# A hybrid encoder trunk: the planner's VectorE costs are refitted

## The chip, the cores and the metric

The kernel runs on one core of one Trainium2 chip, as one program. The metric is device time in microseconds (us) for one execution; the time of a kernel is the median of its runs. The core has TensorE (PE, matrix products, with a queue of its own for loading weights, PEld), VectorE (DVE), ScalarE (ACT), GpSimd (POOL) and SyncE (SP, which only issues DMAs here). Every engine works its own list of instructions in a fixed order and waits on semaphores for what another engine has to deliver.

## The reference

An encoder trunk of two layers on 512 tokens of width 1024, with a memory of 256 tokens. Each layer has four sub-layers, each between a norm ahead of it and a norm behind it:

```python
def rms_norm(x, w):
    xf = x.astype(jnp.float32)
    y = xf * lax.rsqrt(jnp.mean(xf * xf, axis=-1, keepdims=True) + NORM_EPS)
    return (y * w.astype(jnp.float32)).astype(x.dtype)

def swiglu(u, w_gate, w_up, w_down):
    return (jax.nn.silu(u @ w_gate) * (u @ w_up)) @ w_down

# each layer
#   x += 1/2 * postnorm(SwiGLU(prenorm(x)))
#   x +=       postnorm(W_out[ret_heads | gdn_heads](prenorm(x)))
#   x +=       postnorm(CrossAttn(prenorm(x), norm(mem)))
#   x += 1/2 * postnorm(SwiGLU(prenorm(x)))
```

The second sub-layer, called the mixing sub-layer below, has four heads of retention in both directions with rotated queries and keys, and four heads of a gated delta rule whose chunks need a triangular inverse. Everything is float32, and the feed-forward width is 2816.

## The kernel before, in words

**Products.** Each float32 operand of a projection is cut into a high and a low part (`cut`: ScalarE copies the high part, VectorE subtracts it to get the low one), and a product is three matmuls, high by high, high by low and low by high. `uH` and `uL` are the parts of the normalised input `u`, turned so that the model dimension lies on the partitions; `wts` (and `wx` during a transition) are the parts of the weights, cut from the 1 MB blocks `raw` that SyncE loads; `ps` are the eight PSUM banks. These projections run one after the other on TensorE and are called the stream.

**The transition** (`transition`, line 822; `chain`, 758) leads from one sub-layer to the next. The 512 tokens are four tiles of 128, numbered 0 to 3. The output projection finishes tile by tile, and for each tile a thread then does the following:
1. VectorE weighs the output with the post-norm's weights, both halves of 512 columns (`tmp<-ps,wpost`), while ScalarE takes its sum of squares (`junk<-ps`).
2. The inverse root of the mean square (`rsqrt`, small operations on 128x1 tiles `sm`).
3. VectorE updates the residual, half by half (`x<-tmp,sm,x`), and ScalarE takes the sum of squares of each new half (`junk<-x`).
4. A second inverse root, now for the next sub-layer's pre-norm.
5. VectorE makes the next input, half by half (`tmp<-x,sm,wpre`). For each half four transposes on TensorE follow (`ps<-ident,tmp`), and then the cut (`uH<-ps`, `uL<-ps,uH`).

Two tables say which engine takes the roots: `POST_DVE = (3,)` has VectorE take the first root of tile 3 alone, and `PRE_DVE = (0, 1, 3)` has it take the second root of tiles 0, 1 and 3. So both roots of tile 2 are done by GpSimd, 11 operations each (13 with the two that add and scale). The threads' priorities are `PRIO = (-1, -1, 13, -1)`: tile 2 comes last.

Meanwhile the stream goes on with the next sub-layer's first projections (`first_group`, line 734): first for the columns of tiles 0 and 1 (half 0), which need only those two tiles, then for tiles 2 and 3 (half 1), which need both of the others. So half 0 is the work that TensorE has while tiles 2 and 3 are normalised. There are eight such transitions behind a sub-layer, of which seven lead to another sub-layer; the last one only writes the output.

**The mixing sub-layer.** Retention's rotated queries and keys go to memory (`qkd<-rt`) and are loaded again by head (`q<-qkd`, `k<-qkd`), all on SyncE's queue, which also carries the weights (`raw`) and the decay table (`T<-decd`).

**What sets the order.** Every step is written as a thread that yields one operation after the other. `Sched` (line 200 on) runs all threads in a model when the program is built: it holds a clock for each engine and, for each piece of memory, when and by which engine it was written last. `cost` (line 159) estimates how long an operation takes. `ready` (line 216) says when it may start: the writer's end plus `SAME`, if the writer is the same engine, or plus `OTHER` (0.23). `run` (line 276) then takes, on the engine that can start soonest, the operation of the smallest priority number among those that could start within `WAIT` (0.4 us on VectorE) of the earliest. The operations are emitted in that order, and this is the order in which each engine's list stands on the chip. The figures of the model appear nowhere else: they change which operation stands ahead of which, and neither what is computed nor which engine does it.

On the profile nearly all instructions have line 239, the line of the scheduler that emits them, so the groups are told apart by their tiles.

Of the kernel before, what the change touches and what calls it, by code (L numbers as in the profile page):

```python
# [90 lines left out]
class Op:  # L91


    def __init__(self, eng, calls, rd, wr, cost):
        self.eng, self.calls, self.rd, self.wr, self.cost = eng, calls, rd, wr, cost
        self.ready, self.size = 0.0, 0
        self.table = TABLE.get(calls[0][2].get("func")) if eng == "ACT" else None
# [36 lines left out]
def free_size(ap):  # L134
    n = 1
    for _, c in tuple(ap.ap)[1:]:
        n *= c
    return n


class Eng:
# [5 lines left out]
    def __getattr__(self, name):  # L147
        fn, kind = getattr(self.obj, name), self.kind

        def make(*args, **kw):  # L150
            outs = [kw[k] for k in ("out", "accum_out") if kw.get(k) is not None]
            rest = list(args)
            if "out" not in kw:
                outs.append(rest.pop(0))
            ins = [a for a in rest if isinstance(a, bass.AP)]
            ins += [a for k, a in kw.items() if k not in ("out", "accum_out") and isinstance(a, bass.AP)]
            out = outs[0]
            return Op(kind, [(fn, args, kw)], [cells(a) for a in ins], [cells(a) for a in outs],
                      cost(kind, name, out, ins))
        return make  # L160


def cost(kind, name, out, ins):
    n = free_size(out)
    if name == "dma_start":
        return 0.06
    if kind == "PE":
        if name == "transpose":
            return n / 2400 * 2
        if ins[1].dtype == F32R:  # L170
            return max(n, 256) / 2385 if n >= 256 else 0.213
        return 4 * n / 2400
    n = max([n] + [free_size(a) for a in ins])
    psum = any("PSUM" in str(a.space) for a in [out] + list(ins))
    if kind == "ACT":
        return 0.2 + n * 0.00083
    if kind == "DVE":
        if name in ("tensor_copy", "tensor_scalar", "memset") and not psum:
            return 0.07 + n / 1920
        return (0.13 if psum else 0.07) + n / 960  # L180
    if name == "tensor_tensor":
        return 0.15 + n * 0.0036
    return 0.15 + n * 0.0009
# [7 lines left out]


CODE = {"PE": 0, "ACT": 1, "DVE": 2, "POOL": 3, "SP": 4}
SAME, OTHER = 0.12, 0.23
WAIT = {"PE": 0.25, "ACT": 0.3, "DVE": 0.4, "POOL": 0.2, "SP": 0.0}


class Sched:
# [18 lines left out]
    def ready(self, op):  # L217
        e, t = CODE[op.eng], 0.0
        for c in op.rd:
            w, by, r = self.arrays(c)  # L220
            i = slice(None) if c[2] is None else c[2]
            t = max(t, float((w[i] + np.where(by[i] == e, SAME, OTHER)).max()))
            if c[3]:
                t = max(t, float(r[i].max()) + 0.1)
        for c in op.wr:
            w, by, r = self.arrays(c)
            i = slice(None) if c[2] is None else c[2]
            t = max(t, float(r[i].max()) + 0.1)
            if op.eng != "PE" and (c[2] is not None or c[3]):
                t = max(t, float((w[i] + np.where(by[i] == e, 0.0, OTHER)).max()))  # L230
        op.ready = t
# [259 lines left out]
class Kernel:  # L491
# [372 lines left out]
    def ffn(self, l, i, nxt):  # L864
        sd, st = self.sched, self.st
        with self.pool("ffn") as fp:
            h = self.tile(fp, "h", [KF, S])
            hx = [tuple(self.tile(fp, f"hx{c}", [S], F32R) for c in "HL")]
            made, ready = [], set()
            last = [False]  # L870

            first = (l, i) == self.subs[0]
            self.beside = []
            if first:
                self.scratch = h.rearrange("p a b -> p (a b)")
                self.smalls = {n: self.tile(fp, n, [w]) for n, w in (("wm0", KD), ("wm1", KD), ("ms0", 1), ("ms1", 1), ("ms2", 1),
                                                                     ("lg", 16), ("cr", 2))}
                self.beside = [sd.spawn(g, 45, "beside") for g in (self.memory_in(), self.decays_in())]
            self.gate_up(h, made, ready, last, FAST[l, i], nxt, hx)
            th = self.th  # L880
            if first:
                rot = sd.spawn(self.rotary_in(), 45, "rotary")
            self.transition((l, i), nxt, th, True)
            if first:
                sd.run(lambda: rot.done)

    def gate_up(self, h, made, ready, last, j0, nxt, hx):


        sd, st, V = self.sched, self.st, self.V  # L890
        uH, uL = self.uH, self.uL
        plain, formed, done = [False], [False], [False]
        out = lambda k: h[:, k], list(range(KF)), hx + self.uring(), lambda k: k in ready, lambda: last[0]
        gated = {}

# [1042 lines left out]
```

## Time and profile before

| what | value |
|---|---|
| median of 3 runs | 2420.7 us (2415.57 to 2422.01) |
| the profiled execution's own time | 2418.85 us |
| its span in the trace | 2417.1 us |
| mean granted clock of TensorE | 0.996 |
| TensorE busy | 2369.2 us |
| VectorE busy | 1739.7 us |
| ScalarE busy | 1166.0 us |
| GpSimd busy | 197.0 us |

The span runs from the first instruction to the last; the execution's own time is 1.75 us longer. Timeline rows give the start and the duration in us, the engine, the line, the operation, what it writes and reads, its shape and how many were merged; in brackets the idle time of the engine ahead of it and who ended it. Rows of windows give the stretch and its length, the busy time and number of instructions on TensorE, the weight loads, VectorE, ScalarE and GpSimd, then the granted clock of TensorE (1.00 is full), the DMA engines' share and GB/s. Rows of waits give who waited for whom: total us, times, the longest.

### The profile page before, as it was taken

How to read it: one execution, taken by the hardware profiler on the slowest of the kernel's cores; microseconds unless marked ns; L12 is line 12 of the kernel's file. 1: busy time of each engine (PE TensorE's matmuls, PEld its weight loads, DVE VectorE, ACT ScalarE, POOL GpSimd, SP SyncE). 2: the span in 40 equal slices, each digit the busy share in tenths (PEclk: the TensorE clock that was granted, in tenths of full speed). 3: DMA queues.
4: the chain of work that ended last, by engine and by line, in shares of the span. 5: the costliest groups of instructions: out<-in, count | busy, mean ns of one | idle time of the engine just before them, and what ended most of it. 6: DMA issues, size and time to landing. Idle time of an engine off the chain costs nothing. (4 is left out here: it accounts for less than half of the span.)

```text
span 2417.1 us, 38683 instructions
## 1 busy us (share of the span) xinstructions
PE 2369.2 (98%) x15566; PEld 2115.9 (88%) x15566; DVE 1739.7 (72%) x2765; ACT 1166.0 (48%) x2003; POOL 197.0 (8%) x584
## 2 busy tenths in 40 slices
PE   7999999998999999999999999999899999999998
PEld 7999888886989889998889998888788898899987
DVE  7988857767776568886388885486877665788852
ACT  5655436732444544554245563366324454455631
POOL 1000001311020020000010000113010200100001
PEclk9999999999999999999999999999999999999999
DMA  6533342454334322335213334235543253133330
GB/s 202 166 124 108 127 140 88 113 173 152 100 122 159 110 83 81 112 105 174 87 36 107 121 127 153 71 101 142 163 154 136 88 166 105 36 105 117 123 137 35
DMA packets 231209, 286.89 MB, mean 119 GB/s; under 512 B 29630, under 2 KB 190966, under 8 KB 231030
## 3 DMA queue, kind: packets, MB, share of 16 engines
q1 hardware_dynamic: 229878, 280.23, 36.0%
q10 hardware_dynamic: 1152, 4.19, 0.4%
q8 instruction: 122, 2.00, 0.3%
q14 instruction: 57, 0.47, 0.1%
HBM read 255.00 MB, written 29.39 MB: 118 GB/s over the span
## 5 line engine op out<-in xcount | busy, mean ns | idle before, releaser
L239 PE MATMUL ps<-uH,wts 128*128 128x256 f32 (+1 forms) x4096 | 929.8, 313 | 0.0
L239 PEld LDWEIGHTS ps<-uH,wts 128*128 128x128 f32 x4096 | 683.4, 189 | 48.4 <-issue 1.0
L239 PE MATMUL ps<-uL,wts 128*128 128x256 f32 (+1 forms) x2048 | 638.3, 312 | 0.8 <-DVE uL L239 0.8
L239 DVE TENSOR_TENSOR wts<-raw,wts 128x1024 fp32r<-128x1024 f32 (+1 forms) x361 | 403.6, 1126 | 125.8 <-ACT wts L239 125.4
L239 ACT ACTIVATE wts<-raw 128x1024 fp32r<-128x1024 f32 (+1 forms) x361 | 348.1, 971 | 183.4 <-PE ps L239 90.1
L239 PEld LDWEIGHTS ps<-uL,wts 128*128 128x128 f32 x2048 | 386.0, 188 | 25.0 <-DVE uL L239 1.8
L239 PE MATMUL ps<-wts,uH 128*128 128x512 f32 x1120 | 346.8, 391 | 0.0
L239 ACT ACTIVATE sg<-ps 128x256 f32<-128x256 f32 (+1 forms) x298 | 117.6, 397 | 269.4 <-PE ps L239 264.9
L239 PEld LDWEIGHTS ps<-wts,uH 128*128 128x128 f32 x1120 | 208.8, 188 | 42.5
L239 DVE TENSOR_TENSOR wts<-T,wts 128x1024 fp32r<-128x1024 f32 x140 | 171.5, 1225 | 70.8 <-ACT wts L239 66.6
L239 PE MATMUL ps<-wts,uL 128*128 128x512 f32 x560 | 218.2, 390 | 0.0
L239 ACT ACTIVATE wts<-T 128x1024 fp32r<-128x1024 f32 x140 | 148.2, 1058 | 45.2 <-DVE T L239 44.2
L239 PE MATMUL ps<-wx,uH 128*128 128x512 f32 x480 | 148.2, 390 | 0.0
L239 PEld LDWEIGHTS ps<-wts,uL 128*128 128x128 f32 x560 | 105.1, 188 | 22.2
L239 PE MATMUL ps<-s2H,wts 128*128 128x256 f32 x560 | 107.9, 278 | 2.7 <-ACT sg L239 2.7
L239 POOL TENSOR_SCALAR sm<-sm 128x1 f32<-128x1 f32 (+1 forms) x165 | 39.7, 241 | 849.4 <-ACT junk L239 823.9
L239 ACT ACTIVATE uH<-h 128x512 fp32r<-128x512 f32 x76 | 46.3, 626 | 127.2 <-PE ps L239 126.5
L239 PE MATMUL ps<-s3H,wts 128*128 128x256 f32 x560 | 107.6, 277 | 0.0
L239 PE MATMUL ps<-s1H,wts 128*128 128x256 f32 x560 | 107.5, 277 | 0.0
L239 DVE TENSOR_TENSOR uL<-h,uH 128x512 fp32r<-128x512 f32 x76 | 51.2, 689 | 77.2 <-ACT uH L239 77.2
L239 PEld LDWEIGHTS ps<-wx,uH 128*128 128x128 f32 x480 | 89.8, 188 | 18.5
L239 ACT ACTIVATE junk<-ps 128x512 bf16<-128x512 f32 (+1 forms) x96 | 47.0, 490 | 113.0 <-PE ps L239 99.5
(321 smaller groups left out, 4226.1 us busy)
## 6 DMA issues: line engine op xcount, KB each, us to landing
raw<-in_ffn_up_dram SPq DMA_DIRECT2D x44, 1024.0 KB, 5.2
raw<-in_ffn_down_dram SPq DMA_DIRECT2D x44, 1024.0 KB, 4.9
raw<-in_ffn_gate_dram SPq DMA_DIRECT2D x43, 1024.0 KB, 5.2
raw<-in_w_in_dram SPq DMA_DIRECT2D x32, 1024.0 KB, 6.0
raw<-in_w_out_dram SPq DMA_DIRECT2D x8, 1024.0 KB, 5.7
raw<-in_xattn_q_dram SPq DMA_DIRECT2D x8, 1024.0 KB, 5.3
raw<-in_xattn_k_dram SPq DMA_DIRECT2D x8, 1024.0 KB, 5.2
raw<-in_xattn_v_dram SPq DMA_DIRECT2D x8, 1024.0 KB, 5.0
```

What stands on the lines that cost most here:

```text
L239: fn(*a, **kw)
```

## The change

Three figures of the planner are replaced. An operation on VectorE now has a fixed part of 0.155 us, where it had 0.07 (0.13 if it touches PSUM). For VectorE alone the gap between an operation and one that depends on it on the same engine is 0.03 us, where it was 0.12 for every engine; the other engines keep 0.12. The part that grows with the number of elements stays. No thread, priority, tile or operation is edited.

```diff
@@ -176,8 +176,8 @@
     if kind == "DVE":
         if name in ("tensor_copy", "tensor_scalar", "memset") and not psum:
-            return 0.07 + n / 1920
-        return (0.13 if psum else 0.07) + n / 960
+            return 0.155 + n / 1920
+        return 0.155 + n / 960
     if name == "tensor_tensor":
@@ -191,7 +191,7 @@
 CODE = {"PE": 0, "ACT": 1, "DVE": 2, "POOL": 3, "SP": 4}
-SAME, OTHER = 0.12, 0.23
+SAME, OTHER = np.array([0.12, 0.12, 0.03, 0.12, 0.12]), 0.23
 WAIT = {"PE": 0.25, "ACT": 0.3, "DVE": 0.4, "POOL": 0.2, "SP": 0.0}
@@ -219,7 +219,7 @@
             i = slice(None) if c[2] is None else c[2]
-            t = max(t, float((w[i] + np.where(by[i] == e, SAME, OTHER)).max()))
+            t = max(t, float((w[i] + np.where(by[i] == e, SAME[e], OTHER)).max()))
```

In the program that comes out, the operations stand in another order at many places on all engines. The rows of the transition, where the order on VectorE, ScalarE and TensorE changes in the same way seven times, are shown in the prediction.

## The prediction

> **What bounds the kernel now.** I read the page's engine shares first, then the chain of waits, then the timeline of TensorE at its idle places, with ScalarE, VectorE and GpSimd beside it. The page:
>
> ```profile
> span 2417.1 us, 38683 instructions
> PE 2369.2 (98%) x15566; PEld 2115.9 (88%) x15566; DVE 1739.7 (72%) x2765; ACT 1166.0 (48%) x2003; POOL 197.0 (8%) x584
> ```
>
> TensorE is the bound: 2369.2 of 2417.1 us busy, 48 us idle. No order of the other engines can win more than those 48 us, while every place where TensorE comes to wait is paid in full. The view of waits names who makes it wait:
>
> ```profile
> PE ps L239 <- DVE tmp L239: 18.5, 10, 9.3
> PEld ps L239 <- DMA q<-qkd: 13.5, 2, 6.9
> PE ps L239 <- DMA k<-qkd: 12.7, 2, 6.5
> ```
>
> The ten waits for `tmp` are the transitions between sub-layers: 9.3 us of the 18.5 is the start of the program, the rest mostly seven waits of about 1 us, one in each transition with a sub-layer behind it. The two waits for `q` and `k` are the two mixing sub-layers (the weight-load queue and the matmul queue count the same two). A stretch of plain projections shows the stream's own rate:
>
> ```profile
> 966.40:1026.80 60.40, 60.40 (x536) 60.40 (x535) 53.82 (x67) 35.96 (x56) 0.00 (x0) 1.00 0.36 115
> ```
>
> 536 matmuls of 256 columns in 60.40 us are 0.113 us each, with no idle time and the clock at 1.00, though VectorE is 89% busy. Dearer figures for VectorE can win nothing there.
>
> TensorE in the first and the last of the seven: a wait for `uL`, the transposes of token tile 3, then those of tile 2 behind a wait for `tmp`:
>
> ```profile
> 370.57 0.39 PE L239 MATMUL ps<-uL,wts 128*128 128x256 f32 x1 [0.46 <-DVE uL L239]
> 380.60 1.03 PE L239 MATMUL ps<-ident,tmp 128*128 128x128 f32 x8
> 382.57 1.38 PE L239 MATMUL ps<-ident,tmp 128*128 128x128 f32 x8 [0.94 <-DVE tmp L239]
> 383.71 0.36 PE L239 MATMUL ps<-uH,wx 128*128 128x256 f32 x1
> ...
> 2069.74 0.40 PE L239 MATMUL ps<-uL,wx 128*128 128x256 f32 x1 [0.19 <-DVE uL L239]
> 2079.69 1.05 PE L239 MATMUL ps<-ident,tmp 128*128 128x128 f32 x8
> 2081.74 1.38 PE L239 MATMUL ps<-ident,tmp 128*128 128x128 f32 x8 [1.00 <-DVE tmp L239]
> ```
>
> What makes these waits so short is that tile 2's normalisation runs on GpSimd under the stream. Its chain in the first transition, on ScalarE, GpSimd and VectorE:
>
> ```profile
> 375.93 0.63 ACT L239 ACTIVATE junk<-x 128x512 bf16<-128x512 f32 x1
> 376.46 0.19 ACT L239 ACTIVATION_READ_ACCUMULATOR junk<-x 128x1 f32 x1
> ...
> 381.24 1.09 ACT L239 ACTIVATE uH<-ps 128x512 fp32r<-128x512 f32 x2 [2.63 <-PE ps L239]
> 383.27 1.32 ACT L239 ACTIVATE uH<-ps 128x512 fp32r<-128x512 f32 x2 [0.94 <-PE ps L239]
> ```
>
> ```profile
> 365.11 0.27 POOL L239 TENSOR_SCALAR sm<-sm,sm 128x1 f32<-128x1 f32 x1 [1.91 <-ACT junk L239]
> 368.94 0.19 POOL L239 TENSOR_TENSOR sm<-sm,sm 128x1 f32<-128x1 f32 x1
> 376.75 0.92 POOL L239 TENSOR_SCALAR sm<-sm,sm 128x1 f32<-128x1 f32 x1 [7.62 <-ACT junk L239]
> 380.32 0.59 POOL L239 TENSOR_TENSOR sm<-sm 128x1 f32<-128x1 f32 x1
> 381.54 0.19 POOL L239 TENSOR_TENSOR sm<-sm,sm 128x1 f32<-128x1 f32 x1
> ```
>
> ```profile
> 369.16 0.75 DVE L239 SCALAR_TENSOR_TENSOR x<-tmp,sm,x 128x512 f32<-128x512 f32 x1 [1.43 <-POOL sm L239]
> 374.33 2.08 DVE L239 SCALAR_TENSOR_TENSOR x<-tmp,sm,x 128x512 f32<-128x512 f32 x3
> 376.32 1.22 DVE L239 TENSOR_TENSOR wts<-raw,wts 128x1024 fp32r<-128x1024 f32 x1
> 379.44 1.42 DVE L239 SCALAR_TENSOR_TENSOR tmp<-x,sm,wpre 128x512 f32<-128x512 f32 x2
> 381.77 1.41 DVE L239 SCALAR_TENSOR_TENSOR tmp<-x,sm,wpre 128x512 f32<-128x512 f32 x2 [0.91 <-POOL xp L239]
> 383.10 2.48 DVE L239 TENSOR_TENSOR uL<-ps,uH 128x512 fp32r<-128x512 f32 x4
> ```
>
> GpSimd's inverse root (13 operations) takes 4.98 us here, 376.75 to 381.73, of which TensorE waits 0.94. Its first one in this transition took 4.02 (365.11 to 369.13).
>
> **The change part by part.** *The figures themselves* add no instruction. The new ones fit: the 128x1024 operation above takes 1.22 us, 0.155 + 1024/960 = 1.222 against the old 1.137. But no time follows from a better fit; only the order can bring it.
>
> *The transitions.* A shorter gap between dependent operations lets tile 3's small operations (priority -1) follow each other without a hole, so tile 2's update of `x` (priority 13) no longer gets in between. On VectorE, first transition, `x2_8` and `x3_9` are the residual tiles 2 and 3, `tmp_65` and `tmp_66` their work tiles. Before:
>
> ```order
> L239 SCALAR_TENSOR_TENSOR sm3_92_2620<-sm3_93_2621,sm3_92_2620 128x1
> L239 SCALAR_TENSOR_TENSOR x3_9_105<-tmp_66_2583,sm3_92_2620,x3_9_105 128x512
> L239 SCALAR_TENSOR_TENSOR x2_8_104<-tmp_65_2582,sm2_85_2613,x2_8_104 128x512
> L239 SCALAR_TENSOR_TENSOR x3_9_105<-tmp_66_2583,sm3_92_2620,x3_9_105 128x512
> L239 TENSOR_TENSOR wts_84<-raw1_83,wts_84 128x1024
> ```
>
> Now, behind tile 3's second root:
>
> ```order
> L239 SCALAR_TENSOR_TENSOR tmp_66_2577<-x3_9_105,sm3_96_2615,wpre_68_2579 128x512 x2
> L239 SCALAR_TENSOR_TENSOR x2_8_104<-tmp_65_2576,sm2_85_2604,x2_8_104 128x512
> L239 TENSOR_TENSOR uL_2_92<-ps3_77,uH_1_91 128x4x128
> L239 TENSOR_TENSOR uL_2_92<-ps5_79,uH_1_91 128x4x128
> L239 TENSOR_TENSOR wts_84<-raw1_83,wts_84 128x1024
> L239 TENSOR_TENSOR wts_84<-raw0_82,wts_84 128x1024
> L239 SCALAR_TENSOR_TENSOR tmp_65_2576<-x2_8_104,sm2_89_2608,wpre_68_2579 128x512 x2
> ```
>
> Before, the second half of `x2_8` stands between the halves of `x3_9`, ahead of the weight cut and tile 3's second root (its first half stands 15 rows earlier). Now the first half stands there, and the second behind all of that and behind `tmp_66`. On ScalarE, where the sum of squares of that half (`sm2_89`) is taken, before:
>
> ```order
> L239 ACTIVATE junk_73,sm3_95_2623<-x3_9_105 128x512
> L239 ACTIVATE junk_73,sm2_89_2617<-x2_8_104 128x512
> L239 ACTIVATE junk_73,sm3_96_2624<-x3_9_105 128x512
> L239 DMA xd_85<-x3_9_105 128x1024
> L239 DMA xd_85<-x2_8_104 128x1024
> L239 ACTIVATE wts_84<-raw1_83 128x1024
> L239 ACTIVATE uH_1_91<-ps7_81 128x4x128
> L239 ACTIVATE uH_1_91<-ps4_78 128x4x128
> ```
>
> and now:
>
> ```order
> L239 ACTIVATE junk_73,sm2_88_2607<-x2_8_104 128x512
> L239 ACTIVATE junk_73,sm3_96_2615<-x3_9_105 128x512
> L239 DMA xd_85<-x3_9_105 128x1024
> L239 ACTIVATE wts_84<-raw1_83 128x1024
> L239 ACTIVATE uH_1_91<-ps3_77 128x4x128
> L239 ACTIVATE uH_1_91<-ps5_79 128x4x128
> L239 ACTIVATE junk_73,sm2_89_2608<-x2_8_104 128x512
> ```
>
> It has moved behind both copies `uH<-ps` of tile 3, which wait for TensorE's transposes. And those, on TensorE, before:
>
> ```order
> L239 MATMUL ps7_81<-ident_66,tmp_66_2583 128x128 x4
> L239 MATMUL ps4_78<-ident_66,tmp_66_2583 128x128 x4
> L239 MATMUL ps0_74<-ident_66,tmp_65_2582 128x128 x4
> L239 MATMUL ps3_77<-ident_66,tmp_65_2582 128x128 x4
> L239 MATMUL ps5_79<-uH_1_91,wx10_2586 128x256
> ```
>
> and now:
>
> ```order
> L239 MATMUL ps3_77<-ident_66,tmp_66_2577 128x128 x4
> L239 MATMUL ps6_80<-uH_1_91,wx10_2580 128x256
> L239 MATMUL ps6_80<-uL_2_92,wx10_2580 128x256
> L239 MATMUL ps6_80<-uH_1_91,wx10_2580 128x256
> L239 MATMUL ps5_79<-ident_66,tmp_66_2577 128x128 x4
> L239 MATMUL ps0_74<-ident_66,tmp_65_2576 128x128 x4
> L239 MATMUL ps4_78<-ident_66,tmp_65_2576 128x128 x4
> L239 MATMUL ps7_81<-uH_1_91,wts_84 128x256
> ```
>
> Tile 3's transposes now stand at the very end of the first half of the columns (half 0), and nothing is left between them and tile 2's. (Before, twelve matmuls of `wx10` stood behind tile 2's transposes.) The next matmuls, of half 1, need tile 2. So all of tile 2's chain, which lay under the stream, now lies on the path. The same three moves stand in all seven transitions.
>
> Its price, worked out at the first one:
> - TensorE is done with half 0 at 380.60 (where the transposes began before) - 0.46 (the `uL` wait, whose copies now come ahead of the update of `x2_8`) + 12 x 0.113 for the matmuls now ahead of it + 1.03 for tile 3's transposes = 382.5.
> - The second `uH` copy: about 0.65 (half of the 1.32 for two), to 383.2. The sum of squares 0.63 + 0.19, to 384.0. GpSimd starts 0.1 later (376.65 to 376.75): 384.1.
> - GpSimd: 4.02 to 4.98 us, to 388.1 to 389.0. Its slow operations in the rows (0.92, 0.59 against 0.27, 0.19) lie beside VectorE's multiply at 376.32 and `tmp` at 379.44. Now two such multiplies stand beside it; I count the middle.
> - `tmp` half and its way to the transposes: 382.57 - 381.77 = 0.80, so 388.9 to 389.9. Idle 6.4 to 7.4 us; I take 6.9. An earlier VectorE can't shorten it: the place in ScalarE's queue sets it.
> - Behind the transposes the copies `uH`, `uL` of tile 2 are now uncovered: four transposes, then 0.65 + 0.62 (a quarter of 2.48) of copies, about 0.9 us of it behind the other four transposes. Before, the twelve matmuls hid them.
> - The clock. After the 6.5 us stall of the mixing sub-layer it is halved, after the 1 us wait of a transition it isn't:
>
> ```profile
> 2080.00:2081.70 1.70, 0.74 (x7) 0.47 (x5) 0.79 (x3) 1.09 (x2) 0.65 (x4) 1.00 0.00 0
> 2081.70:2083.00 1.30, 1.16 (x9) 0.95 (x10) 1.30 (x3) 0.57 (x1) 0.00 (x0) 1.00 0.00 0
> ```
>
> ```profile
> 552.70:553.70 1.00, 0.92 (x1) 0.50 (x2) 0.93 (x3) 0.59 (x1) 0.00 (x0) 0.50 0.02 5
> ...
> 554.70:555.70 1.00, 1.00 (x3) 0.48 (x2) 0.90 (x4) 0.00 (x0) 0.00 (x0) 0.50 0.00 0
> 555.70:556.70 1.00, 1.00 (x3) 0.47 (x3) 0.87 (x4) 0.00 (x0) 0.00 (x0) 0.98 0.00 0
> ...
> 1746.20:1748.20 2.00, 1.96 (x3) 0.96 (x4) 1.83 (x6) 0.54 (x1) 0.00 (x0) 0.50 0.04 10
> 1748.20:1750.20 2.00, 2.00 (x4) 0.89 (x3) 1.76 (x8) 0.00 (x0) 0.00 (x0) 0.50 0.00 0
> 1750.20:1752.20 2.00, 2.00 (x6) 0.91 (x5) 1.93 (x6) 0.00 (x0) 0.00 (x0) 0.95 0.00 0
> ```
>
> Half rate for 2.9 us after the first stall (552.8 to 555.7), 4.0 after the second (1746.2 to 1750.2): a loss of 1.5 to 2.0 us. In a transition about 1 us of it falls on the wait for the copies, so I count 1.2. The Trainium skill ("TensorE: Matmul & The Clock Gate", What's actually happening) has the gate close after an idle window of about 3.4 us that runs freely, and open after as long a busy one. By it a gap of 6.9 us always holds one whole window, so it always halves, at 1.7 us, or 3.5 us more in all seven than my sum; gaps of 3.4 to 6.8 would halve in some transitions only. The trace has no gap of that middle size, so no run here shows that part.
>
> Taken off: the wait of 0.94 to 1.00 (0.97) and the `uL` wait (0.46 at the first, 0.19 at the last, so 0.2). Per transition 6.9 + 0.9 + 1.2 - 0.97 - 0.2 = 7.8 us; seven make 55 us. Bounds: without any clock loss and copies' wait, with GpSimd at 4.02 us, 6.4 - 1.2 = 5.2, so 36; with 7.4 + 1.3 + 2.0 - 1.2 = 9.5, so 67.
>
> *The mixing sub-layers.* The first layer's stall, SyncE's row and TensorE's:
>
> ```profile
> 545.13 0.38 SPq L239 DMA_DIRECT2D raw<-in_w_in_dram  x1
> 545.57 0.57 SPq L239 DMA_DIRECT2D q<-qkd  x1
> ```
>
> ```profile
> 552.78 2.05 PE L239 MATMUL ps<-q,k 128*128 128x512 f32 x2 [6.49 <-DMA k<-qkd]
> ```
>
> SyncE's row still is: the decay table, 1 MB of weights, `q`, `k`, `v`. In the first layer they stand as far from TensorE's first `q`, `k` product as before, but the chunk inverse starts later and the first values product stands behind 7 us more of stream: between 0 and +6. In the second layer the row is issued 3.2 us of stream earlier, so the stall there (6.2 to 6.9 us) shrinks to about 3, and its clock loss may go: between 0 and -6. Together I take 0, from -6 to +6.
>
> *The feed-forward sub-layers.* VectorE's and ScalarE's rows change places by a few, TensorE's stream doesn't, and it didn't wait there (first window above): 0, from -1 to +3.
>
> Sum, against the profiled execution's own time of 2418.85 us (1.75 above its span; the median of the runs is 1.85 higher, 2420.7): 2418.85 + 55 + 0 = 2474 us.
>
> **The rivals.**
> 1. *The chain stays partly covered.* For: tile 2's other half is done earlier and ScalarE reaches the queue early. Against: nothing of the stream is left by TensorE's row. If GpSimd and the copies overlap better than any row shows, 4 us a transition: 2418.85 + 28 = 2447.
> 2. *Faster, the other side:* the one mechanism is that tile 2's chain is hidden after all, because TensorE reaches the end of half 0 late, held up for as long as the chain takes (6.9 us) by something else, such as the weights. Then only what is taken off counts: 7 x 1.17 = 8, and the second layer's stall, 3.2: 2408. It decides only if TensorE has other work or other waits past 382.5, and no row shows any.
> 3. *It doesn't do what it says:* the rows move but each engine's slack swallows it, TensorE waits as before: 2419. VectorE's idle quarter speaks for it, the places where TensorE waits against it.
> 4. *Slower still:* the first layer's inverse comes on the path (+6) and the clock is halved for 4 us in all transitions, with the copies' 1.3: 2418.85 + 67 + 6 = 2492.
>
> **How the numbers follow.** The forecast and its own bounds have 0.75, rival 4 beyond it 0.06, rival 1 0.08, rival 3 0.05, rival 2 0.06. The range of 80% takes the forecast's bounds (36 to 67, with the mixing's -6 to +6) and reaches into rivals 1 and 4: 2445 to 2494. A measurement of this kernel tells 0.3% (7 us) from no change: its three runs lie within 6.4 us. Faster by more than that: 0.06; within: 0.05; slower: 0.89.
>
> **What would show it.** In the changed kernel's waits, TensorE for `tmp` (or its weight loads) rises from 18.5 to about 60 us, with seven waits of 6 to 7.5. GpSimd's root for tile 2 starts about 384 instead of 376.75 in the first transition, after the copies of `uH`. The clock reads 0.50 for some 3 us behind each. Copies `uL` make TensorE wait 0.9 there. I am wrong if the waits in the transitions stay at 1 us, if the clock stays at 1.00 behind them, or if the mixing sub-layers hold more than 10 us of the difference.

## The result, and the profile after

The changed kernel takes 2509.2 us (median of 4 runs, 2502.0 to 2513.9) where the kernel before took 2418.8 on the same chip: 1.038 times as long, interval 1.036 to 1.040. The forecast was 2474 with a range up to 2494: the sign was right, the size too small by 35 us.

The page of the changed kernel (its profiled execution took 2513.9 us), and what TensorE waited for:

```profile
span 2512.1 us, 38568 instructions
PE 2403.2 (96%) x15566; PEld 2147.7 (85%) x15566; DVE 1752.8 (70%) x2765; ACT 1154.2 (46%) x1997; POOL 199.1 (8%) x584
PEclk9989999998999999999999999999979999999999
...
PE ps L239 <- DVE tmp L239: 68.4, 12, 8.8
```

The spans differ by 95.0 us. TensorE's idle time has grown from 47.9 to 108.9 (span less busy time), which is 61.0; the other 34.0 are busy time, for the same 15566 matmuls. They are longer where the clock is lower, and the clock's row is no longer all nines. So there are two losses to explain, and waits are only the larger one.

TensorE's row in the first transition, with tile 3's transposes and then tile 2's, and below it tile 2's in the fourth transition:

```profile
395.53 0.60 PE L239 MATMUL ps<-ident,tmp 128*128 128x128 f32 x4
403.96 1.97 PE L239 MATMUL ps<-ident,tmp 128*128 128x128 f32 x8 [7.83 <-DVE tmp L239]
...
1288.75 1.97 PE L239 MATMUL ps<-ident,tmp 128*128 128x128 f32 x8 [8.69 <-DVE tmp L239]
```

All seven transitions have this wait, five of 7.83 and two of 8.69 us: 56.5 us, where before it was 6.8. Its chain stands as the prediction's order has it. ScalarE, GpSimd and VectorE in the first one:

```profile
396.16 0.60 ACT L239 ACTIVATE uH<-ps 128x512 fp32r<-128x512 f32 x1 [0.20 <-PE ps L239]
396.66 0.62 ACT L239 ACTIVATE junk<-x 128x512 bf16<-128x512 f32 x1
397.18 0.19 ACT L239 ACTIVATION_READ_ACCUMULATOR junk<-x 128x1 f32 x1
```

```profile
397.47 2.33 POOL L239 TENSOR_SCALAR sm<-sm,sm 128x1 f32<-128x1 f32 x1 [14.26 <-ACT junk L239]
...
402.92 0.19 POOL L239 TENSOR_TENSOR sm<-sm,sm 128x1 f32<-128x1 f32 x1
```

```profile
393.96 0.74 DVE L239 SCALAR_TENSOR_TENSOR x<-tmp,sm,x 128x512 f32<-128x512 f32 x1
397.40 2.35 DVE L239 TENSOR_TENSOR wts<-raw,wts 128x1024 fp32r<-128x1024 f32 x2
403.15 1.41 DVE L239 SCALAR_TENSOR_TENSOR tmp<-x,sm,wpre 128x512 f32<-128x512 f32 x2 [3.40 <-POOL xp L239]
```

From TensorE's last transposes (396.13) it is 1.2 us to the end of the sum of squares, 5.6 us for GpSimd's root, and 0.8 to tile 2's transposes. Tile 2's half of `x` was there at 394.7: it lay waiting behind ScalarE's copies.

Two places were not in the forecast. In the first feed-forward sub-layer TensorE stands still twice:

```profile
126.58 1.97 PE L239 MATMUL ps<-ident,h 128*128 128x128 f32 x8 [6.28 <-DVE h L239]
135.56 0.58 PE L239 MATMUL ps<-s2H,wts 128*128 128x256 f32 x1 [7.01 <-ACT sg L239]
```

And in the mixing sub-layers the waits for `q` and `k` have become shorter (4.06 and 0.81 us, where they were 6.5 and 6.2), but the clock is at half for long stretches in the chunk inverse. In both layers a short wait stands at its start: 2.52 us in the first, with half clock for the 20.5 us behind it, and these two in the second:

```profile
1831.64 0.66 PE L239 MATMUL ps<-ident,xc 128*128 128x128 f32 x4 [1.15 <-DVE xc L239]
...
1834.55 1.17 PE L239 MATMUL ps<-Tb,Am 32*32 32x32 f32 x32 [1.10 <-DVE Tb L239]
```

Windows of the changed kernel there (columns: TensorE, weight loads, VectorE, ScalarE, GpSimd, clock, DMA), and of the second layer's inverse before:

```profile
1821.90:1836.10 14.20, 11.92 (x126) 8.98 (x126) 9.10 (x20) 3.75 (x11) 0.00 (x0) 1.00 0.80 229
1836.10:1866.80 30.70, 30.70 (x321) 26.82 (x318) 13.47 (x24) 3.96 (x12) 8.31 (x8) 0.50 0.13 42
1866.80:1872.00 5.20, 5.20 (x37) 3.54 (x37) 3.04 (x8) 0.00 (x0) 0.00 (x0) 1.00 0.02 3
```

```profile
1772.30:1798.00 25.70, 25.68 (x436) 21.67 (x436) 19.59 (x34) 4.99 (x13) 8.31 (x8) 1.00 0.17 51
```

TensorE is busy in the whole stretch of 30.7 us, with no wait to be seen, and does 321 matmuls where 436 went through in 25.7 before. Its 32x32 matmuls start 0.051 us apart (0.031 before), the 64x64 ones 0.095 (0.058). At the distances of before the stretch would take some 17 us, by estimate: some 13 us lost that no list of waits shows.

### The profile page after: what moved, and what is told of

It is laid out like the page before. It is cut to its first block, busy times and chain, and to the rows that moved or that the text cites. A ratio compares the mean times of both kernels' runs of the same rounds, so it can differ in the third digit from the quotient of the medians.

```text
span 2512.1 us, 38568 instructions
## 1 busy us (share of the span) xinstructions
PE 2403.2 (96%) x15566; PEld 2147.7 (85%) x15566; DVE 1752.8 (70%) x2765; ACT 1154.2 (46%) x1997; POOL 199.1 (8%) x584
## 5 line engine op out<-in xcount | busy, mean ns | idle before, releaser
L239 DVE TENSOR_TENSOR wts<-T,wts 128x1024 fp32r<-128x1024 f32 x140 | 171.3, 1224 | 25.8 <-ACT wts L239 23.9
L239 PE MATMUL ps<-s2H,wts 128*128 128x256 f32 x560 | 108.9, 279 | 7.0 <-ACT sg L239 7.0
L239 PE MATMUL ps<-ident,tmp 128*128 128x128 f32 x256 | 45.7, 318 | 68.5 <-DVE tmp L239 68.4
```

The lines of the kernel that those rows point to most:

```text
L239: fn(*a, **kw)
```

## The experiments

All kernels compute the encoder, but for the clock probe. The ratio is to the kernel before on the same chip, with its 95% interval.

| kernel | us | ratio |
|---|---|---|
| new figures in transitions only | 2451.7 | 1.0144 (1.0124 to 1.0163) |
| new figures everywhere else | 2447.5 | 1.0125 (1.0108 to 1.0142) |
| in the first feed-forward sub-layer only | 2433.1 | 1.0063 (1.0048 to 1.0078) |
| in the mixing sub-layers only | 2441.2 | 1.0107 (1.0081 to 1.0133) |
| fixed part only | 2508.7 | 1.0365 (1.0340 to 1.0391) |
| gap only | 2432.7 | 1.0055 (1.0040 to 1.0071) |
| changed, tile 2's priority -1 | 2455.2 | 1.0139 (1.0108 to 1.0171) |
| changed, tile 2's root on VectorE | 2483.5 | 1.0252 (1.0225 to 1.0280) |
| before, 0.07 for PSUM | 2427.6 | 1.0044 (1.0029 to 1.0059) |
| before, tile 2's root on VectorE | 2430.5 | 1.0058 (1.0040 to 1.0076) |
| changed, 16 large matmuls in each inverse | 2519.6 | 1.0406 (1.0388 to 1.0425) |
| changed, 48 large matmuls in each inverse | 2515.6 | one run |
| before, `q` and `k` ahead of the weights | 2417.2 | 0.9991 (0.9979 to 1.0003) |

**Where the time goes: the figures switched by stage.** A flag says which figures the planner uses, and stages set it:

```diff
+NEW, SAME, OTHER = [False], np.array([[0.12] * 5, [0.12, 0.12, 0.03, 0.12, 0.12]]), 0.23
+        fixed = 0.155 if NEW[0] else 0.13 if psum else 0.07
     def transition(self, sub, nxt, stream, half=False, initial=False):
+        kept, NEW[0] = NEW[0], True
...
+        NEW[0] = kept
```

Transitions only:

> The new figures hold only while a transition is planned (from the down or output projection to the end of the next first projections); everywhere else the old ones. In five of the seven transitions tile 2's second half of x now stands behind tile 3's tmp, in the two behind a mixing sub-layer it does not. Theory (each transition so ordered puts tile 2's chain on the path, 8 to 9 us with its clock loss, whatever lies ahead of it): 5 x 8.9 = 44 us over before, about 2463 us, five waits for tmp of 7.8 to 8.7 us and two of about 1 us. Rival (the waits come from the sub-layers ahead running late): within 5 us of before, 2419.

Everything else:

> The reverse: the new figures everywhere but in the transitions. Theory (transitions about 62 of the 90 us, the first feed-forward sub-layer 15, the two mixing sub-layers the rest): 2509 - 62, about 2447 us, all waits for tmp behind the start about 1 us. Rival (the transitions' waits come from what lies ahead of them): 2490 or more.

The first feed-forward sub-layer only:

> The new figures only in the first feed-forward sub-layer up to its transition. Theory (the memory's transposes now stand on TensorE ahead of work that is ready, 13 us of waits and 3 us of half clock): about 2418.8 + 15 = 2434 us with two waits of 6 to 7 us between 110 and 140 us. Rival (the planner's different start makes them, not the figures in this stage): 2419 and no such wait.

The mixing sub-layers only:

> The new figures only in the two mixing sub-layers up to their transitions. Theory (the small matmuls of the chunk inverse stand together behind short waits, and the clock stays at half through them): half clock for 20 to 31 us at each inverse, and 20 to 25 us over before in all, about 2441 us. Rival (the clock was lost through the waits of the transitions ahead): no half clock at the inverse, 2419.

Measured: 2451.7, 2447.5, 2433.1 and 2441.2 us. With the old figures in the transitions the changed kernel loses 2509.2 - 2447.5 = 61.7 us of its time; the first feed-forward sub-layer alone costs 14.8 and the mixing sub-layers alone 22.9 (over 2418.3). The three make 99, nine more than the whole. The first run shows why it isn't simply a sum: its five long waits should cost 44 us and it is 33 slower, and its stalls for `q` and `k` have shrunk from 6.5 and 6.2 to 0.95 us and nothing. TensorE comes to the first of these products 9.2 us later than in before, and the transfer lands only 3.6 us later, so part of a transition's wait is given back at the next stall. The two transitions that kept their order in that kernel waited 1.73 us each, the five others 7.4 to 8.7. So the first run missed its number and bears out its mechanism; the other three met their times within 1 us, but not every detail: the first feed-forward sub-layer alone has one long wait and not two, and the half clock at the second inverse lasts 17.1 us, where 20 to 31 were expected.

In the first feed-forward sub-layer's own kernel the wait is one of 13.90 us. TensorE, ScalarE and VectorE there:

```profile
135.57 0.58 PE L239 MATMUL ps<-s2H,wts 128*128 128x256 f32 x1 [13.90 <-ACT sg L239]
```

```profile
135.13 0.66 ACT L239 ACTIVATE sg<-ps 128x256 f32<-128x256 f32 x2 [0.24 <-DVE h L239]
```

```profile
132.03 0.69 DVE L239 TENSOR_SCALAR h<-h,lg 128x896 f32<-128x896 f32 x1 [2.04 <-DMA decd<-h]
132.75 1.15 DVE L239 SCALAR_TENSOR_TENSOR h<-h,lg 128x896 f32<-128x896 f32 x1
133.82 1.22 DVE L239 TENSOR_TENSOR h<-sg,sg 128x1024 f32<-128x1024 f32 x1
```

The product `h<-sg,sg`, on which the next gates and TensorE wait, stands on VectorE behind side work for later layers (the retention decays `h<-h,lg` of 896 columns), one step of which itself waits for a DMA to leave its buffer. It stands behind three pairs of these operations from 123.5 on; in before it ran at 119.84, behind one pair. In the changed kernel, too, it runs at 133.80 behind three pairs. That this order is the cause is read from these rows; the side work was not moved by itself. The cause that the expectation named, the memory's transposes `ps<-ident,h` on TensorE, does not fit: here four of the sixteen stand on TensorE just ahead of the waiting matmul, without a wait of their own (in the changed kernel eight, with the wait of 6.28).

**Which of the two figures.** Each alone, in the whole program:

```diff
-SAME, OTHER = np.array([0.12, 0.12, 0.03, 0.12, 0.12]), 0.23
+SAME, OTHER = np.array([0.12, 0.12, 0.12, 0.12, 0.12]), 0.23
```

> Only the fixed part of 0.155 us; the gap between dependent operations stays 0.12 on VectorE too. Theory A (the longer fixed part is what moves tile 2's second half of x behind tile 3: it does so in all seven transitions of this order): seven long waits, 2490 to 2525 us. Theory B (as the prediction has it, the shorter gap moves it): transitions as before, 2419 to 2445 us.

and the old fixed parts with the new gap:

> Only the gap of 0.03 us between dependent operations on VectorE; the fixed parts stay as they were. Theory A (the fixed part is the cause): the transitions' order is that of before, waits of about 1 us, within 12 us of 2419. Theory B (the shorter gap is the cause): 2480 us or more.

2508.7 and 2432.7 us. The waits of TensorE for `tmp`, in the first and in the second of these kernels:

```profile
PE ps L239 <- DVE tmp L239: 66.7, 11, 8.6
```

```profile
PE ps L239 <- DVE tmp L239: 20.9, 19, 9.2
```

The longer fixed part alone makes the whole loss, and with the shorter gap alone the transitions keep their order. Theory A holds for the transitions, and the prediction's reading of the planner falls. The 15 us that the gap alone does cost, just beyond the 12 that theory A allowed, are again the first feed-forward sub-layer (a wait of 7.73 us for `s2H`, from 121.8 on), small waits, and half clock for 6.8 and 10.2 us at the two inverses (3.4 us and none in before).

**What in the transition.** The changed kernel with another priority for tile 2, and with tile 2's second root on another engine:

```diff
-PRIO = (-1, -1, 13, -1)
+PRIO = (-1, -1, -1, -1)
```

> The changed kernel with tile 2's priority set from 13 to -1, that of the other tiles: both halves of its x now come ahead of tile 3's in all seven transitions. Theory (the transitions' 62 us come from tile 2's place in the order alone): waits of 1 us or so in the transitions, 2509 - 62, about 2447 us, the rest as in the changed kernel. Rival (whichever tile comes last pays the same): 2490 us or more, with waits of 4 us and up for tile 3.

```diff
-PRE_DVE = (0, 1, 3)
+PRE_DVE = (0, 1, 2, 3)
```

> The changed kernel with tile 2's second root on VectorE instead of GpSimd; its place in the order stays. Theory (GpSimd's root, 5.6 us in the changed kernel, is most of the wait of 7.8): VectorE's ten operations take about 2 us, so each wait falls to about 4 us, 7 x 3.8 = 27 us less and up to 15 us of half clock less: 2467 to 2482 us. Rival (the place behind ScalarE's copies and the weight cuts sets the wait): waits over 6 us, 2495 us or more.

2455.2 and 2483.5 us. With tile 2 ahead of tile 3 the long waits are gone; what is left is waits of 0.3 to 2.3 us for `uL`, which explains most of the 8 us above the expected 2447. With the root on VectorE the waits fall to 4.07 us, as worked out, but the clock still halved behind all seven, for 6.83 us in six of them and 3.41 in the first. The work at half clock behind the waits even grew from 32 to 40 us in all, so the gain of up to 15 us did not come, and 26 of the changed kernel's us went instead of 27 to 42. So the place in the order makes the wait, and GpSimd's root is half of its length.

The same edit in the kernel before:

> The kernel before with tile 2's second root on VectorE instead of GpSimd. Theory (in before the transitions' last wait of 0.97 us is for GpSimd's root): seven waits gone or halved, 3 to 7 us faster, 2411 to 2416 us. Rival (VectorE becomes the one waited for): the waits stay at 1 us or grow, 2418 to 2435 us.

2430.5 us: the rival. The waits of 1 us have grown to 1.75 to 1.79 in all seven, since the root now queues on VectorE behind tile 3's, and the waits for `uL` have grown with them (6.3 us in all). In sum TensorE is idle only 4.6 us longer than in before, because the stalls for `q` and `k` are all but gone (0.3 us). The larger part of the loss is the clock: 33 us of TensorE's work at half clock instead of 10.5, behind four of the seven transitions among other places.

**The figure itself.** In the prediction's rows of before four `uL` operations take 2.48 us together, and the last of them lasts 0.69: they start 0.60 apart. So such an operation on PSUM keeps VectorE for 0.07 + 512/960, though it is shown for 0.155 + 512/960; the end of one lies under the start of the next. The old figure of 0.07 is that distance, and 0.07 + 0.12 is the 0.19 between dependent operations of one element. The new pair has the same sum for a dependent operation (0.185), and lies 0.085 us above the distance of independent ones. (Not all kinds have this distance: `x<-tmp,sm,x` of the same size, which takes a factor per row, starts 0.67 apart, which is 0.135 + 512/960.) If so, 0.07 should serve for PSUM too:

```diff
-        return (0.13 if psum else 0.07) + n / 960
+        return 0.07 + n / 960
```

> The kernel before with one figure changed: 0.07 instead of 0.13 us as the fixed part of VectorE's operations on PSUM, since the trace of before starts independent operations of 128x512 0.60 us apart (0.07 + 512/960) though each is shown for 0.68. Theory (what the planner needs is the distance between starts, not the shown duration): no slower than before, 2400 to 2422 us, waits of 1 us or less in the transitions. Rival (any other figure throws the hand-fitted order off): 2440 us or more.

2427.6 us, 0.44% slower: between theory and rival. The transitions are as good as before's and the stalls for `q` and `k` shrink to 2.42 and 1.65, but the wait for `s2H` in the first feed-forward sub-layer is there with 7.67 us (7 us or more, as in every kernel here whose figures differ in that stage), and the clock is at half for 13.7 and 10.2 us at the two inverses, 3.4 us and none in before. A figure that is nearer to the chip did not give a better order here.

**The clock.** A kernel of matmuls alone:

> Nothing of the encoder is computed: TensorE alone runs stretches of float32 matmuls on one tile, and zeros are written out. Order: 30 of 128x512, 700 of 32x32 directly behind, 30 of 128x512; a wait of about 6 us, 700 of 32x32, 30 of 128x512; the same wait, 300 of 64x64, 30 of 128x512; the same wait, 120 of 128x128, 30 of 128x512; a wait of about 3 us, 700 of 32x32, 30 of 128x512; a wait of about 3 us, 30 of 128x512. Theory (small matmuls don't open the clock again once a wait has halved it): half rate through the whole 32x32 stretch behind the long wait, more than 20 us, and full again only within the large ones that follow; 128x128 opens it after 3 to 7 us. Rival (busy time alone counts, whatever the matmul's size): full again 3 to 7 us into every stretch.

Its windows (TensorE, weight loads, VectorE, GpSimd, clock, DMA): large matmuls, the 32x32 ones behind them without a wait, large ones again; then 64x64 behind a wait of 6.6 us, then 128x128 behind the same wait:

```profile
4.00:32.00 28.00, 28.00 (x60) 12.09 (x60) 1.40 (x2) 0.00 (x0) 1.00 0.20 75
32.10:35.60 3.50, 3.50 (x112) 3.50 (x112) 0.00 (x0) 0.00 (x0) 1.00 0.02 5
35.70:104.40 68.70, 68.70 (x1292) 68.69 (x1289) 0.00 (x0) 0.00 (x0) 0.50 0.01 2
104.50:107.30 2.80, 2.80 (x5) 1.25 (x5) 0.00 (x0) 0.00 (x0) 0.50 0.00 0
107.40:131.80 24.40, 24.40 (x57) 10.50 (x56) 0.00 (x0) 0.00 (x0) 1.00 0.00 1
...
247.60:311.60 64.00, 64.00 (x600) 63.99 (x600) 0.00 (x0) 0.00 (x0) 0.50 0.01 1
346.30:349.60 3.30, 3.30 (x16) 3.30 (x17) 0.00 (x0) 0.00 (x0) 0.50 0.00 0
349.70:374.70 25.00, 25.00 (x226) 25.00 (x226) 0.00 (x0) 0.00 (x0) 1.00 0.01 1
```

More than the theory asked for: for the clock, matmuls of 32x32 and 64x64 look like idle time. Straight behind large ones and with TensorE busy throughout, the clock halves 3.5 us into them and stays so for 69 us, until 2.9 us of large ones have run. 128x128 ones open it after 3.4 us. The rival is out.

In the changed kernel, extra large matmuls ahead of eight steps of each inverse, two at each (16 in each inverse; the expectation's count of 32 is that of both):

```diff
             px = bk.view(16, 32)
+            yield join(*[self.mm(bk.t, self.uH[:, 0, 0:P], self.uH[:, 0]) for _ in range(2)])
```

> The changed kernel with 32 extra matmuls of 128x512 (0.23 us each at full rate) in each chunk inverse, two ahead of each of its steps' first product and of the level-1 steps' second; their results are overwritten. Theory (large matmuls in each 3.4 us stretch keep the clock, small ones alone lose it, also in this kernel): half clock at the two inverses falls from 20.5 and 30.7 us to under 7 each, worth 18 to 22 us; the extra matmuls cost 2 x 5 us or so where they don't fill waits: 2490 to 2502 us. Rival (the clock is lost through the waits at the inverse's start and comes back when it will): half clock stays at 20 us or more in each, 2515 us or more.

2519.6 us, and half clock for 23.9 and 20.5 us: the theory as put there failed, and the rival's numbers came. The clock was lost with the wait at the inverse's start (in the first layer 2.53 us, up to 595.72, with half clock from 596.0 on), and two matmuls at each place didn't bring it back. Then six at each:

> As the run with extra matmuls, but six of 128x512 instead of two at each of the eight places in each chunk inverse (48 in each; the run before had two at each, 16 in each, none ahead of the level-1 steps' second products as its text says). Theory (a share of large matmuls decides): each place now holds 1.4 us of large matmuls at full rate, or 2.8 at half, beside 1.2 to 3.5 us of small ones, so that the clock comes back early: half clock under 10 us at each inverse. Rival (only 3.4 us of nothing but large ones brings it back): 20 us or more at each.

Windows over the inverses, of the kernel with two (the first layer's), and of that with six (both layers'):

```profile
596.10:619.80 23.70, 23.70 (x293) 20.09 (x292) 10.94 (x14) 3.54 (x6) 6.01 (x6) 0.50 0.20 69
```

```profile
598.90:602.20 3.30, 3.30 (x14) 2.12 (x12) 2.94 (x3) 0.93 (x2) 0.00 (x0) 0.50 0.23 96
602.30:626.00 23.70, 23.70 (x367) 20.42 (x365) 13.47 (x21) 4.13 (x13) 9.29 (x8) 1.00 0.17 55
1835.60:1860.00 24.40, 24.34 (x361) 20.56 (x362) 15.25 (x20) 5.16 (x14) 9.29 (x8) 1.00 0.30 98
```

With six the clock is back after one stretch of 3.4 us in the first layer and is never lost in the second, with the same small matmuls between: under 10 us, as the theory has it.

What the share does can be counted. All changes of the clock within a trace lie on one grid of 3.41 us, so each step of the grid can be taken for itself, with the share of it in which matmuls of 128x128 and larger ran. With six, the step that brought the clock back had a share of 0.92, and steps of 0.41 to 0.69 behind it kept it. In the kernel before, steps down to 0.14 kept it in the second inverse, and one of 0.11 lost it for a step in the first. With two, steps of up to 0.62 didn't bring it back; 0.72 and 0.86 did (in the changed kernel 0.72 did once and failed once). So a smaller share keeps the clock than brings it back, and two at each place were too few for the second. The exact border was not tried. As a cure six cost what they bring: 2515.6 us, one run, against 2509.2.

**The stalls for `q` and `k`.** SyncE's order in the kernel before, with the loader held until head 0's `v` is issued:

> The kernel before; SyncE issues q, k and v of the first retention head ahead of the 1 MB of weights that stood ahead of them, once in each mixing sub-layer, nothing else moves on SyncE. Theory (the 6.5 us stalls for q and k are the 1 MB transfer in front): they land about 4 us earlier, the planner lets TensorE reach them 2.7 us earlier: stalls of 4 to 5 us, 2 to 5 us gained in all, 2412 to 2415 us. Rival (the wait is for the last rotated keys to be written): stalls of 6 us or more, 2417 to 2422 us.

2417.2 us, ratio 0.9991 (0.9979 to 1.0003): not to be told from before, and neither the theory's 2412 to 2415 nor the rival's stalls. Counted from the transition ahead, `q` and `k` land 3.4 and 4.5 us earlier, and TensorE reaches them 2.7 us earlier, as planned; the stalls are 5.76 and 4.43 us. Some 2.5 us are left to gain in both together. No version here beats the kernel before.

## Why the prediction was wrong

**What held.** TensorE is the bound, and places where it waits are paid in full. The transitions are the largest part, through the three moves that the order shows: 61.7 us when they are taken out of the changed kernel, 55 forecast, within its bounds of 36 to 67 (the new figures in the transitions only, where five of the seven have this order, cost 33).

**The sum of a transition**, term by term at the first one. The sum of squares was done 1.2 us behind the transposes, 1.5 forecast. GpSimd's root took 5.6 us, and 4.0 to 5.0 was taken: its first operation, 0.92 beside one weight cut of VectorE before (a subtraction; the prediction calls it a multiply), took 2.33 beside two. I had the row that pointed there and counted the middle instead of the upper end or beyond. So the wait was 7.83 and not 6.9. The copies' wait of 0.9 was hardly there (the waits for `uL` hold 0.4 us in all, and that at 25.8, ahead of all seven). The clock term was too small: 1.2 us counted, and at the first transition the clock is at half for 5.2 us of TensorE's work behind the wait, which is 2.6:

```profile
403.90:409.30 5.40, 5.20 (x22) 4.67 (x23) 2.04 (x3) 1.19 (x2) 0.65 (x3) 0.50 0.01 3
409.30:411.00 1.70, 1.70 (x16) 1.70 (x16) 0.00 (x0) 0.34 (x1) 0.00 (x0) 0.99 0.00 0
```

In all seven it is at half for 3.7 to 5.4 us behind the wait, 16 us lost where 8 were counted. The prediction's estimate from the Trainium skill ("TensorE: Matmul & The Clock Gate", What's actually happening), 1.7 us a transition, was nearer than mine and still short. By the free-running window of about 3.4 us that the Trainium skill states there, a wait of 4.07 us need not halve the clock; with tile 2's root on VectorE it did, behind all seven. That the trace has no gap of 3.4 to 6.8 us, as I wrote, was a slip: the stalls of 6.49 and 6.22 us are such gaps, and both halved the clock.

**"The feed-forward sub-layers: 0, from -1 to +3" failed**, by 14.8 us. I took TensorE's row to be the same there, and looked at a stretch without side work. The first feed-forward sub-layer has side work on VectorE and ScalarE, and it was the order there that changed who is late; on TensorE, too, eight transposes of the memory had moved (the wait of 6.28).

**"The mixing sub-layers: together 0, from -6 to +6" failed**, by 22.9 us. That the second layer's stall shrank (from 6.2 to 0.81, 3 forecast) was luck: SyncE's row alone does not do it, for with the new figures in the mixing sub-layers only it is 5.96, while with the new figures in the transitions only it is gone. What failed is that TensorE's row was taken as time: the inverse's small matmuls had moved together behind a short wait, and each then takes 1.6 times as long, because too few large ones stand between to bring the clock back. The prediction had the clock as a price of long waits only. Its own sign of being wrong, more than 10 us in the mixing sub-layers, came.

**The planner's mechanism failed**: it is the longer fixed part that moves tile 2's half behind tile 3, not the shorter gap. This changed no number, since the order was read and not derived, but it would have led to the wrong cure.

Of the rivals none came: the chain wasn't covered, nothing else held TensorE up, and the slower one, with 2492 the nearest, had the clock behind the waits about right (4 us) but the inverse at 6 us for a wait, not at more than 20 for the clock.

## What to carry to other kernels

A cost model that is to be true to the chip takes the distance from one start to the next, once for independent and once for dependent operations; durations in a timeline overlap (0.68 us shown, 0.60 apart) and are not occupancy. That truer figures alone give a faster order, no run here shows. When an order changes, price it at each place where the engines that feed the bound carry more than one job, and not only in the stretch where the bound waits today. And a busy engine isn't a fast one: the granted clock belongs beside each stretch, with the size of the matmuls in it.

## What the runs showed of the hardware

- Small matmuls don't hold TensorE's clock: 32x32 and 64x64 in float32 ran at half clock for 69 and 64 us on end, 128x128 opened it in 3.4 us. In the inverses a smaller share of large matmuls kept the clock (0.14 in one step of 3.41 us) than brought it back (0.72 to 0.92).
- A wait of 2.97 us with large matmuls behind it still cost 3.41 us of half clock in the probe (the clock is 0.57 over the 4.0 us behind it):

```profile
509.50:513.50 4.00, 4.00 (x6) 1.69 (x7) 0.00 (x0) 0.00 (x0) 0.57 0.00 0
```

- A GpSimd operation on 128x1 elements took 2.33 us beside two 128x1024 subtractions on VectorE, in all seven transitions; 0.87 to 0.93 beside one in before, and 0.27 without (the prediction's row at 365.11).
